# Input projection of the Mamba-2 layer: operand halves side by side, normalized inputs, half-size units, two evacuation queues

## The chip, the cores and the metric

One core of one Trainium2 chip runs the whole program in one launch. The metric is device microseconds (us) of one execution, the median of three runs.

## The reference, cut to what matters

A two-layer trunk on 256 tokens with width 2048. Layer 0 is a Mamba-2 mixer, layer 1 windowed attention, and each is followed by a SwiGLU FFN. The change touches only the first step of layer 0:

```python
h = rms_norm(x, mix_norm[0])          # x * rsqrt(mean(x*x) + eps) * gain
proj = h @ w_in                       # 2048 -> 10304
z   = proj[..., :4096]
xbc = silu(causal_depthwise_conv(proj[..., 4096:10240], conv_w, conv_b))   # x, B, C
dt  = softplus(proj[..., 10240:] + dt_bias)
# then per group (8 of them): SSD over 8 heads, y * silu(z), RMS norm, @ w_out
```

## The kernel before, in words

**Split arithmetic.** Each fp32 operand is held as a high part and a low part, and a product is the sum of high·high, high·low and low·high on TensorE (PE). Weights arrive in tiles of 128x2048; each half of a tile (128x1024) is split on the chip by `split` (L145): a ScalarE (ACT) cast makes `wh`, a VectorE (DVE) subtraction makes `wl`. Both have four buffers, and `next_half` (L160) issues splits three halves ahead of their use. A *half* below is one such piece and the matmuls that read it.

**Units.** A unit fills one of two accumulators `acc` (two PSUM banks each). `t_units` (L222) runs three passes over 256 columns: high weights on the activation's high part, on its low part, and low weights on the high part, 24 matmuls a half. `p_unit` (L250) streams high and low parts side by side, so that a high weight tile is loaded once for 512 columns: 8 matmuls of 512 (L261) and 8 of 256 (L265) a half. It leaves two sums that have to be added afterwards. The FFN and half of the output projection use `p_unit` already.

**Work behind the matmuls.** What follows a unit is a Python generator, put in a queue of `Background` (L43). After each half `step` (L68) advances the front generator of each queue by one piece, unless the work issued on DVE or ACT exceeds its allowance (1.3 and 1.4 us a half, by the kernel's own estimate); what exceeds it stays as a debt. The order of every engine's instructions is fixed by this when the program is built. `begin_unit` (L199) may have two units open: before a new one starts, `need` (L74) advances all queues, whatever the debt, until the unit two before it has been evacuated, so that its accumulator is free. Instructions issued there stand ahead of the new unit's matmuls, and on DVE and ACT ahead of the next split.

**The projection** (L633 to L643): per group g one unit for B and C (256 columns, 4 halves), one for x (512 columns, 8 halves), one for z (8 halves); in group 0 also dt (2 halves). The inputs `XT` are x times gain, without the RMS factor; `scaled` (L392) multiplies that factor `rb` in when it reads PSUM, so no evacuation can start before the norm of all inputs is known (`prep`, L377). `bc_evac`, `x_evac` and `z_evac` go to queue 0, `dt_evac` and `ssd` to queue 2, `ssd_norm` to queue 1.

Of the kernel before, what the change touches and what calls it, by code (L numbers as in the profile page):

```python
# [10 lines left out]
F32 = mybir.dt.float32  # L11
F32R = mybir.dt.float32r
AF = mybir.ActivationFunctionType
OP = mybir.AluOpType
# [71 lines left out]
def trunk_kernel(  # L86
# [41 lines left out]
    def bg_bank():  # L128
        return psum.tile([P, 512], F32, tag="bg", bufs=4, name=name("bg"))

    bg = Background(3, (V, A))


    n_tiles = weights.shape[0]
# [112 lines left out]
    def t_unit(ncols, X, xkey, evac, q=0):  # L247
        t_units([(0, range(16))], ncols, 16, X, xkey, [evac], q)

    def p_unit(nk, X, xkey, evac):  # L250


        u, ps = begin_unit()
        for k0 in range(0, nk, 4):
            h, l = next_half(256)
            ks = range(k0, k0 + 4)
            for k in ks:
                bg.need((xkey, k // 2))
            for k in ks:
                for m in range(2):  # L260
                    T.matmul(ps[:, m], h[:, k % 4, m * P:(m + 1) * P], X[k], start=(k == 0), stop=False,  # L261
                             skip_group_check=True)
            for k in ks:
                for m in range(2):
                    T.matmul(ps[:, m, 0], l[:, k % 4, m * P:(m + 1) * P], X[k][:, 0, :], start=False,  # L265
                             stop=(k == nk - 1), skip_group_check=True)
            bg.step()
        bg.add(0, evac(ps, u))

    def joined(ps):  # L270

# [105 lines left out]
    def prep():  # L377
        for nb in range(4):
            for pair in (2 * nb, 2 * nb + 1):
                gained(pair, 0)  # L380
            add_squares()
            for pair in (2 * nb, 2 * nb + 1):
                squares(pair)
            yield
        yield from finish_norm()
        V.tensor_scalar(cwb, cwb, 0.5, None, OP.mult)
        A.activation(hpar[64:128, 1:2], hpar[64:128, 1:2], AF.Exp)
        V.tensor_scalar(hpar[64:128, 1:2], hpar[64:128, 1:2], -1.0, None, OP.mult)
        V.memset(hpar[0:64, 1:2], 1.0)
        bg.done.add("prep")  # L390

    def scaled(sums):  # L392
        u = tmp([P, 2, S])
        V.tensor_tensor(u, sums, rb[:, None, :].to_broadcast([P, 2, S]), OP.mult)
        return u

    def dt_evac(ps, u):
        while "prep" not in bg.done:
            yield
        xb, e, r, q = (wide()[:, 0:S] for _ in range(4))  # L400
        V.tensor_tensor(xb, ps[:, 0, 0], rb, OP.mult)
        bg.done.add(("evac", u))
        A.activation(xb, xb, AF.Identity, bias=hpar[:, 0:1])
        A.activation(e, xb, AF.Abs)
        A.activation(e, e, AF.Exp, scale=-1.0)
        yield
        V.tensor_scalar(r, e, 2.0, None, OP.add)
        V.reciprocal(r, r)
        yield
        V.tensor_tensor(e, e, r, OP.mult)  # L410
        V.tensor_tensor(r, e, e, OP.mult)
        yield
        V.tensor_scalar(q, r, 1.0 / 19, None, OP.mult)
        for j, c in enumerate((17, 15, 13, 11, 9, 7, 5, 3)):
            V.scalar_tensor_tensor(q, q, 1.0 / c, r, OP.add, OP.mult)
            if j % 2:
                yield
        V.scalar_tensor_tensor(q, q, 1.0, e, OP.add, OP.mult)
        V.tensor_scalar(xb, xb, 0.0, None, OP.max)
        V.scalar_tensor_tensor(q, q, 2.0, xb, OP.mult, OP.add)  # L420
        V.tensor_scalar(q, q, hpar[:, 1:2], None, OP.mult)
        yield
        b = bg_bank()
        for tb in range(2):
            T.transpose(b[:, tb * P:(tb + 1) * P], q[:, tb * P:(tb + 1) * P], ident)
        yield
        bv = b[:, 0:256].rearrange("p (t d h) -> p t d h", d=2, h=64)
        an = tmp([P, 2, 64])
        V.tensor_copy(dtn, bv[:, :, 0, :])
        V.tensor_copy(an, bv[:, :, 1, :])  # L430
        yield
        b1, b2 = bg_bank(), bg_bank()
        for c in range(2):
            T.matmul(b1[0:64, c * P:(c + 1) * P], an[:, c, :], tri, start=(c == 0), stop=True, skip_group_check=True)
        for j, (lhs, c) in enumerate(((tri, 0), (tri2, 0), (tri, 1))):
            T.matmul(b2[:, j * 64:(j + 1) * 64], lhs, an[:, c, :], start=(j == 0), stop=True, skip_group_check=True)
        yield
        at = tmp([P, S])
        V.tensor_copy(at[0:64, :], b1[0:64, 0:256])
        nc.gpsimd.dma_start(acum, at[0:64, :])  # L440
        for j, sc in enumerate((1.0, -1.0, 1.0)):
            A.mul(bias3[:, j, :], b2[:, j * 64:(j + 1) * 64], sc)
        yield
# [11 lines left out]
                V.scalar_tensor_tensor(dst[:, m, d:], u[:, m, :S - d], cwb[:, j * 48 + ct:j * 48 + ct + 1],  # L455
                                       dst[:, m, d:], OP.mult, OP.add)

    def half_tanh(v, scale):
        th = tmp([P, 2, S])
        A.activation(th, v, AF.Tanh, scale=scale)  # L460
        return th

    def gate(out_, th, v):
        V.scalar_tensor_tensor(out_, th, 1.0, v, OP.add, OP.mult)

    def bc_evac(g):
        def gen(ps, u):
            v = scaled(ps[:, :, 0])
            bg.done.add(("evac", u))
            yield  # L470
            both, cts = slot([P, 1024]), (32 + g, 40 + g)
            bc = both[:, 0:512].rearrange("p (a t) -> p a t", t=S)
            first_tap(v, bc, cts)
            yield
            taps(v, bc, cts, (2, 1))
            yield
            taps(v, bc, cts, (0,))
            yield
            th = half_tanh(bc, 1.0)
            yield  # L480
            gate(bc, th, bc)
            BC[g] = bc, both[:, 512:896]
            yield
        return gen

    def x_evac(g):
        def gen(ps, u):
            xs = slot([P, 4, S])
            d0, d1 = xs[:, 0:2, :], xs[:, 2:4, :]
            c0, c1 = (4 * g, 4 * g + 1), (4 * g + 2, 4 * g + 3)  # L490
            v0 = scaled(ps[:, 0])
            yield
            first_tap(v0, d0, c0)
            v1 = scaled(ps[:, 1])
            bg.done.add(("evac", u))
            yield
            taps(v0, d0, c0, (2, 1))
            first_tap(v1, d1, c1)
            yield
            taps(v0, d0, c0, (0,))  # L500
            taps(v1, d1, c1, (2,))
            yield
            th = half_tanh(d0, 1.0)
            taps(v1, d1, c1, (1, 0))
            yield
            gate(d0, th, d0)
            th = half_tanh(d1, 1.0)
            yield
            gate(d1, th, d1)
            XS[g] = xs  # L510
            bg.add(2, ssd(g))
        return gen

    def z_evac(g):
        def gen(ps, u):
            sz = slot([P, 4, S])
            v0 = scaled(ps[:, 0])
            yield
            t0 = half_tanh(v0, 0.5)
            v1 = scaled(ps[:, 1])  # L520
            bg.done.add(("evac", u))
            yield
            gate(sz[:, 0:2, :], t0, v0)
            t1 = half_tanh(v1, 0.5)
            yield
            gate(sz[:, 2:4, :], t1, v1)
            SZ[g] = sz
        return gen

    BC, XS, SZ, Y = {}, {}, {}, {}  # L530

    def ssd(g):
# [31 lines left out]
        def gated(b):  # L564
            if gates[0] > b:
                return True
            if g not in SZ:
                return False
            sz = SZ[g] if b == 0 else SZ.pop(g)
            for i in range(2):  # L570
                p = 2 * b + i
                V.scalar_tensor_tensor(xs[:, p, :], xs[:, p, :], dsk[:, 4 * g + p:4 * g + p + 1],
                                       yb[b][:, i * S:(i + 1) * S], OP.mult, OP.add)
            G.tensor_tensor(xs[:, 2 * b:2 * b + 2, :], xs[:, 2 * b:2 * b + 2, :], sz[:, 2 * b:2 * b + 2, :], OP.mult)
            gates[0] += 1
            return True
# [28 lines left out]
            yield  # L605
        while not gated(1):
            yield
        bg.add(1, ssd_norm(g, xs))

    def ssd_norm(g, xs):  # L610
        sq = [tmp([P, 2, S]) for _ in range(2)]
        for b in range(2):
            A.activation(sq[b], xs[:, 2 * b:2 * b + 2, :], AF.Square)
        yield
# [15 lines left out]
            store(Y, 4 * g + 2 * i, t)  # L630
            bg.done.add(("Y", 2 * g + i))

    bg.add(0, prep())  # L633
    bg.need(("XT", 1))
    for g in range(NG):
        t_unit(256, XT, "XT", bc_evac(g))
        if g == 0:
            t_unit(128, XT, "XT", dt_evac, 2)
        t_unit(512, XT, "XT", x_evac(g))
        t_unit(512, XT, "XT", z_evac(g))  # L640
    bg.need("rstd")
    bg.need(("evac", units[0] - 1))
    clear_norm()  # L643
    t_units(OUT0, 512, 32, Y, "Y", [t_residual(nb, 32) for nb in (0, 1)])
    for pair in range(4, 8):
        p_unit(32, Y, "Y", p_residual(pair, 32))
# [255 lines left out]
def _weights(i):  # L902
# [15 lines left out]
    for g in range(NG):  # L918
        put(r16, (w_in, 8192 + g * P, P), (w_in, 9216 + g * P, P))
        if g == 0:  # L920
            put(r16, (w_in, 10240, 64), (w_in, 10240, 64))
        put(r16, (w_in, 4096 + g * 512, 512))
        put(r16, (w_in, g * 512, 512))

    def put_out(w, order, nk):
        for j, ks in order:
# [85 lines left out]
```

## Time and profile before

| | |
|---|---|
| median of 3 runs (range) | 2697.92 us (2697.36 to 2698.32) |
| the profiled execution | 2698.51 us |
| its span on the engines | 2696.4 us |
| PE, PE weight loads, DVE, ACT busy | 99%, 89%, 63%, 49% of the span |
| granted PE clock over the span | 0.999 of full speed |

The projection takes the first 0.5 ms or so, the output projection of layer 0 runs from about 570 to 632 us, and the FFN follows. Times in the rows are us from the start of the span; a matmul's row gives the time that it was in the engine, and since matmuls overlap, the pace is read from the starts.

### The profile page before, as it was taken

How to read it: one execution, taken by the hardware profiler on the slowest of the kernel's cores; microseconds unless marked ns; L12 is line 12 of the kernel's file. 1: busy time of each engine (PE TensorE's matmuls, PEld its weight loads, DVE VectorE, ACT ScalarE, POOL GpSimd, SP SyncE). 2: the span in 40 equal slices, each digit the busy share in tenths (PEclk: the TensorE clock that was granted, in tenths of full speed). 3: DMA queues.
4: the chain of work that ended last, by engine and by line, in shares of the span. 5: the costliest groups of instructions: out<-in, count | busy, mean ns of one | idle time of the engine just before them, and what ended most of it. 6: DMA issues, size and time to landing. Idle time of an engine off the chain costs nothing.

```text
span 2696.4 us, 40315 instructions
## 1 busy us (share of the span) xinstructions
PE 2673.5 (99%) x16460; PEld 2391.9 (89%) x16460; DVE 1700.7 (63%) x2104; ACT 1326.3 (49%) x1947; POOL 199.8 (7%) x215
## 2 busy tenths in 40 slices
PE   7999999999999999999999999999999999999999
PEld 7999999999888888888888888888888888888888
DVE  6777777756566666665555777766666666665444
ACT  5666666654454444444444555544454444444332
POOL 1011111110000000000001330220000000000000
PEclk9999999999999999999999999999999999999999
DMA  5454555545555555555555554553455555555553
GB/s 222 178 184 175 187 179 189 177 177 187 188 188 188 188 188 187 189 189 193 190 189 203 183 186 152 185 185 141 156 188 188 188 188 188 188 188 194 197 198 128
DMA packets 71432, 495.75 MB, mean 184 GB/s; under 512 B 8320, under 2 KB 8704, under 8 KB 13008
## 3 DMA queue, kind: packets, MB, share of 16 engines
q1 hardware_dynamic: 68400, 483.81, 49.5%
q0 software_dynamic: 2848, 9.37, 1.1%
q8 instruction: 129, 2.11, 0.3%
q14 instruction: 55, 0.45, 0.1%
HBM read 490.99 MB, written 2.16 MB: 183 GB/s over the span
## 4 chain that ended last, share of the span: by engine, by line
PE 98%; ACT 1%; issue 0%; DVE 0%; POOL 0%; DMA 0%; SPq 0%; ACTq 0%; POOLq 0%
PE acc L261 39%; PE acc L240 21%; PE acc L265 20%; PE acc L217 15%; PE bg L588 1%; PE bg L754 0%; PE bg L787 0%; PE bg L860 0%; PE bg L549 0%; ACT wh L38 0%; ACT slot L38 0%; PE bg L324 0%; PE bg L784 0%; PE bg L862 0%; DMA xres<-in_x_dram 0%
## 5 line engine op out<-in xcount | busy, mean ns | idle before, releaser
L38 DVE TENSOR_TENSOR wl<-w,wh 128x1024 fp32r<-128x1024 f32 x914 | 1128.3, 1236 | 904.7 <-ACT wh L38 903.7
L38 ACT CAST wh<-w 128x1024 fp32r<-128x1024 f32 x914 | 955.5, 1047 | 1089.8 <-PE acc L261 507.2
L261 PE MATMUL acc<-slot,wh 128*128 128x512 f32 x4416 | 1106.7, 392 | 2.1 <-DVE xres L38 1.7
L261 PEld LDWEIGHTS acc<-slot,wh 128*128 128x128 f32 x4416 | 794.2, 189 | 145.1 <-issue 2.7
L265 PEld LDWEIGHTS acc<-slot,wl 128*128 128x128 f32 x4416 | 602.4, 190 | 43.0
L265 PE MATMUL acc<-slot,wl 128*128 128x256 f32 x4416 | 615.7, 282 | 0.0
L240 PE MATMUL acc<-slot,wh 128*128 128x256 f32 x3232 | 430.1, 286 | 12.8 <-ACT wh L38 10.7
L240 PEld LDWEIGHTS acc<-slot,wh 128*128 128x128 f32 x3232 | 404.8, 193 | 19.9 <-ACT wh L38 10.8
L217 PE MATMUL acc<-wh,slot 128*128 128x512 f32 x1152 | 290.5, 394 | 0.0
L217 PEld LDWEIGHTS acc<-wh,slot 128*128 128x128 f32 x1152 | 213.7, 188 | 43.2
L240 PE MATMUL acc<-slot,wl 128*128 128x256 f32 x1616 | 226.8, 283 | 0.9 <-DVE wl L38 0.9
L240 PEld LDWEIGHTS acc<-slot,wl 128*128 128x128 f32 x1616 | 208.6, 192 | 1.1 <-DVE wl L38 1.1
L217 PE MATMUL acc<-wl,slot 128*128 128x512 f32 x576 | 154.2, 389 | 0.0
L217 PEld LDWEIGHTS acc<-wl,slot 128*128 128x128 f32 x576 | 108.1, 188 | 22.7
L38 ACT ACTIVATE tmp<-tmp 128x256 f32<-128x256 f32 (+1 forms) x104 | 46.8, 450 | 163.9 <-DVE tmp L38 163.6
L284 POOL TENSOR_TENSOR tmp<-tmp 128x256 f32<-128x256 f32 x32 | 27.6, 868 | 1022.1 <-ACT tmp L38 1017.0
L38 ACT ACTIVATE wide<-tmp,bias 128x128 f32<-128x128 f32 x192 | 62.9, 391 | 13.9 <-PE bg L588 9.4
L38 DVE SCALAR_TENSOR_TENSOR slot<-tmp,vec,slot 128x255 f32<-128x255 f32 (+1 forms) x144 | 67.6, 528 | 0.0
L38 DVE TENSOR_TENSOR tmp<-tmp 128x256 f32<-128x256 f32 x88 | 37.4, 425 | 42.6 <-ACT tmp L38 42.6
L38 DVE TENSOR_TENSOR tmp<-acc,tmp 128x512 f32<-128x512 f32 x88 | 60.1, 683 | 4.0 <-ACT tmp L38 4.0
L38 DVE TENSOR_TENSOR tmp<-tmp,rb 128x512 f32<-128x512 f32 x88 | 60.3, 686 | 0.1
L38 ACT ACTIVATE tmp<-slot 128x128 f32<-128x128 f32 (+1 forms) x136 | 52.7, 394 | 14.9 <-DVE slot L38 13.8
(131 smaller groups left out, 1191.3 us busy)
## 6 DMA issues: line engine op xcount, KB each, us to landing
w<-in_weights_dram SPq DMA_DIRECT2D x455, 1024.0 KB, 4.8
tmp<-acum POOLq DMA_DIRECT2D x32, 256.0 KB, 4.6
xres<-in_x_dram SPq DMA_DIRECT2D x4, 512.0 KB, 7.8
w<-in_weights_dram SPq DMA_DIRECT2D x4, 512.0 KB, 8.4
out_dram<-xres SPq DMA_DIRECT2D x8, 256.0 KB, 2.2
slot<-in_mask_dram POOLq DMA_DIRECT2D x1, 384.0 KB, 5.6
slot<-in_q_norm_dram POOLq DMA_DIRECT2D x1, 192.0 KB, 5.6
slot<-in_k_norm_dram POOLq DMA_DIRECT2D x1, 192.0 KB, 7.5
```

The costliest lines, as they stand in the source:

```text
L38: return call(out, *args, **kw)
L217: T.matmul(ps[tb], X[k][:, part, tb * P:(tb + 1) * P], w[:, k % 2, :], start=(k == 0 and i == 0), stop=(k == 15 and i == 2))
L240: T.matmul(pss[j][:, b, c, :], w[:, k % kk, m * P:(m + 1) * P], X[k][:, part, :], start=(k == 0 and i == 0 and c == 0), stop=(k == nk - 1 ...
L261: T.matmul(ps[:, m], h[:, k % 4, m * P:(m + 1) * P], X[k], start=(k == 0), stop=False, skip_group_check=True)
L265: T.matmul(ps[:, m, 0], l[:, k % 4, m * P:(m + 1) * P], X[k][:, 0, :], start=False, stop=(k == nk - 1), skip_group_check=True)
L284: G.tensor_tensor(sq[:, 0, :], sq[:, 0, :], sq[:, 1, :], OP.add)
L588: T.matmul(o[:, tb * P:], xdt[:, tb, q * 64:(q + 1) * 64], m[:, 256 * tb:256 + 128 * tb], start=(tb == 0 and q % 4 < 2), stop=(tb == 1), s ...
```

## The change

- The projection's units become `p_unit`s of 256 columns, 4 halves each: per group B/C, x first half, z first half, x second half, z second half. dt stays a `t_unit`. The weights are packed in that order.
- For groups 1 to 7 the operands are `XN`: x·gain·rb, made by a new generator `normed` after `prep`. Only group 0 still reads `XT` and multiplies by `rb` when it is evacuated.
- `total` takes a unit out of PSUM: an ACT copy of the second sum, and, one step later, a DVE addition of the first. `conv` holds the convolution, one engine's work in each step. `z_evac` has one step for the tanh and one for the product.
- B/C and z evacuations go to a fourth queue (number 3), x evacuations to queue 0, `prep` to queue 1. `ssd_norm` squares into z's buffer instead of two temporary ones.

```diff
-    bg = Background(3, (V, A))
+    bg = Background(4, (V, A))
...
-        bg.add(0, evac(ps, u))
+        bg.add(q, evac(ps, u))
...
+    def normed():
...
+            if j >= 2:
+                v, t = vs.pop(j - 2), ts.pop(j - 2)
+                V.tensor_tensor(t[:, :, 1, :], v, t[:, :, 0, :].bitcast(F32), OP.subtract)
...
+            if 1 <= j < 9:
+                ts[j - 1] = operand()
+                A.copy(ts[j - 1][:, :, 0, :], vs[j - 1])
+            if j < 8:
+                v = vs[j] = tmp([P, 2, S])
+                for i in range(2):
+                    k = 2 * j + i
+                    V.scalar_tensor_tensor(v[:, i, :], xt[:, k, :], gains[:, k:k + 1], rb, OP.mult, OP.mult)
+            yield
+
+    def total(ps, u, g):
+        v = tmp([P, 2, S])
+        A.copy(v, ps[:, :, 1])
+        yield
+        V.tensor_tensor(v, ps[:, :, 0], v, OP.add)
+        bg.done.add(("evac", u))
+        if g == 0:
+            while "prep" not in bg.done:
+                yield
+            V.tensor_tensor(v, v, rb[:, None, :].to_broadcast([P, 2, S]), OP.mult)
+        yield
+        return v
...
     def dt_evac(ps, u):
+        xb, e, r, q = (wide()[:, 0:S] for _ in range(4))
+        A.copy(xb, ps[:, 0, 0])
+        bg.done.add(("evac", u))
         while "prep" not in bg.done:
             yield
...
+    def conv(u, dst, cts):
+        first_tap(u, dst, cts)
+        yield
+        taps(u, dst, cts, (2, 1))
+        yield
+        taps(u, dst, cts, (0,))
+        yield
+        A.activation(u, dst, AF.Tanh)
+        yield
+        gate(dst, u, dst)
...
     for g in range(NG):
-        t_unit(256, XT, "XT", bc_evac(g))
+        X, key = (XT, "XT") if g == 0 else (XN, "XN")
+        p_unit(16, X, key, bc_evac(g), 3)
         if g == 0:
             t_unit(128, XT, "XT", dt_evac, 2)
-        t_unit(512, XT, "XT", x_evac(g))
-        t_unit(512, XT, "XT", z_evac(g))
-    bg.need("rstd")
+        for i in range(2):
+            p_unit(16, X, key, x_evac(g, i))
+            p_unit(16, X, key, z_evac(g, i), 3)
```

How the instructions move is seen at two places. Halves are counted from 1 through the projection, 162 in all. Names with numbers are buffers: `acc_65`, `acc_82` and `acc_108` are the units of halves 11 to 14, 15 to 18 and 19 to 22 after the change, `wl` the low weights of a half, `slot_79` and `slot_100` convolution results, `wide` values of the dt chain, `rb` the RMS factor.

DVE before, in the middle of the second unit of 512 columns (halves 15 to 22), where the dt chain ends:

```order
L38 TENSOR_TENSOR wl_83_683<-w_67_548,wh_82_682 128x1024
L38 TENSOR_TENSOR tmp_84_712<-acc_50_384,rb_97 128x512
L38 SCALAR_TENSOR_TENSOR wide_49_379<-wide_49_379,wide_47_377 128x256
L38 TENSOR_SCALAR wide_46_376<-wide_46_376 128x256
L38 SCALAR_TENSOR_TENSOR wide_49_379<-wide_49_379,wide_46_376 128x256
L38 TENSOR_SCALAR wide_49_379<-wide_49_379,vec_77 128x256
L38 TENSOR_TENSOR wl_86_719<-w_67_548,wh_85_718 128x1024
L38 SCALAR_TENSOR_TENSOR slot_79_675<-tmp_80_676,vec_77,slot_79_675 128x255 x2
L38 SCALAR_TENSOR_TENSOR slot_79_675<-tmp_80_676,vec_77,slot_79_675 128x254 x2
L38 TENSOR_TENSOR wl_89_755<-w_73_614,wh_88_754 128x1024
```

DVE with the change, the end of what `need` issues ahead of half 19 (the 44 instructions from the split of half 21 to the addition that empties `acc_65`), and what follows:

```order
L38 SCALAR_TENSOR_TENSOR slot_100_669<-tmp_47_335,slot_100_669 128x512
L38 SCALAR_TENSOR_TENSOR wide_46_333<-wide_46_333,wide_44_331 128x256
L38 TENSOR_SCALAR wide_43_330<-wide_43_330 128x256
L38 SCALAR_TENSOR_TENSOR wide_46_333<-wide_46_333,wide_43_330 128x256
L38 TENSOR_SCALAR wide_46_333<-wide_46_333,vec_77 128x256
L38 SCALAR_TENSOR_TENSOR slot_79_545<-tmp_97_659,slot_79_545 128x512
L38 TENSOR_TENSOR tmp_106_720<-acc_65_449,tmp_106_720 128x512
L38 TENSOR_TENSOR tmp_106_720<-tmp_106_720,rb_97 128x512
L38 TENSOR_TENSOR wl_110_730<-w_76_523,wh_109_729 128x1024
L38 TENSOR_TENSOR wl_113_752<-w_85_579,wh_112_751 128x1024
L38 TENSOR_TENSOR wl_115_772<-w_85_579,wh_114_771 128x1024
```

Before, two to five instructions stand between one split and the next. With the change 45 stand between the splits of halves 21 and 22, and then eight splits follow each other.

PE with the change, from the end of half 18 into half 19:

```order
L265 MATMUL acc_82_554<-slot_27_222,wl_84_556 128x256 x4
L265 MATMUL acc_82_554<-slot_28_227,wl_84_556 128x256 x4
L456 MATMUL bg_107_723<-cm_75,wide_46_333 128x128 x2
L261 MATMUL acc_108_728<-slot_4_101,wh_86_581 128x512 x4
L261 MATMUL acc_108_728<-slot_5_106,wh_86_581 128x512 x4
L265 MATMUL acc_108_728<-slot_4_101,wl_87_582 128x256 x4
```

Half 19 writes the accumulator that `acc_65` held, and stands behind the transposes (L456) of the dt chain's last `wide_46`.

ACT with the change, what `need` issues ahead of half 31 (`acc_140` is the unit of halves 27 to 30, `acc_119` that of 23 to 26, which half 31 waits for):

```order
L38 CAST wh_149_1001<-w_127_876 128x1024
L38 COPY tmp_151_1021<-acc_140_936 128x512
L38 COPY slot_100_669<-bg_137_921 128x128
L38 ACTIVATE slot_131_901<-tmp_135_917 128x512
L38 ACTIVATE wide_154_1033<-tmp_136_919,bias3_99 128x128 x3
L38 ACTIVATE wide_154_1033<-wide_154_1033 128x384
L38 ACTIVATE slot_155_1039<-tmp_151_1021,vec_77 128x256 x2
L38 ACTIVATE wide_156_1043<-tmp_136_919,bias3_99 128x128 x3
L38 ACTIVATE wide_156_1043<-wide_156_1043 128x384
L38 COPY tmp_158_1050<-acc_119_813 128x512
```

The copy of the unit that has just ended now stands first, and the copy that frees the accumulator last.

## Rows read from the trace of the kernel before

**Rows 1.** The page: busy time of the engines and its share of the span.

```profile
PE 2673.5 (99%) x16460; PEld 2391.9 (89%) x16460; DVE 1700.7 (63%) x2104; ACT 1326.3 (49%) x1947; POOL 199.8 (7%) x215
```

**Rows 2.** Stretches: length, busy PE, PEld, DVE, ACT, POOL, clock, DMA share, GB/s.

```profile
300.00:360.00 60.00, 60.00 (x500) 58.09 (x499) 46.17 (x69) 36.39 (x61) 10.04 (x11) 1.00 0.51 183
700.00:900.00 200.00, 200.00 (x1147) 176.01 (x1146) 123.30 (x144) 95.32 (x125) 3.60 (x5) 1.00 0.51 185
```

**Rows 3.** PE's timeline in the projection: start, us; two halves of 24 matmuls.

```profile
42.11 2.08 PE L240 MATMUL acc<-slot,wh 128*128 128x256 f32 x16
44.99 2.08 PE L240 MATMUL acc<-slot,wh 128*128 128x256 f32 x16
```

**Rows 4.** The timeline in the FFN: two starts of a half, and a split.

```profile
699.02 1.05 ACT L38 CAST wh<-w 128x1024 fp32r<-128x1024 f32 x1 [1.74 <-PE acc L261]
699.77 2.00 PE L261 MATMUL acc<-slot,wh 128*128 128x512 f32 x8
700.10 1.23 DVE L38 TENSOR_TENSOR wl<-w,wh 128x1024 fp32r<-128x1024 f32 x1 [1.57 <-ACT wh L38]
...
702.56 2.00 PE L261 MATMUL acc<-slot,wh 128*128 128x512 f32 x8
```

**Rows 5.** The timeline where the norm of the inputs is awaited.

```profile
31.72 0.51 PE L311 MATMUL bg<-ones,rb 128*128 128x2 f32 x4
...
34.57 1.22 PE L324 MATMUL bg<-tmp,ones 128*128 128x256 f32 x2 [2.35 <-POOL tmp L321]
...
36.72 0.69 DVE L38 TENSOR_TENSOR tmp<-acc,rb 128x512 f32<-128x512 f32 x1
...
37.56 3.75 PE L240 MATMUL acc<-slot,wh 128*128 128x256 f32 x16 [1.77 <-DVE tmp L38]
```

**Rows 6.** Stretches inside and behind that pause; the clock is third from the end.

```profile
33.00:34.00 1.00, 0.00 (x0) 0.00 (x0) 0.00 (x0) 0.00 (x0) 0.90 (x3) 1.00 0.98 393
38.00:39.00 1.00, 1.00 (x7) 1.00 (x7) 0.00 (x0) 0.94 (x3) 0.00 (x0) 0.50 0.00 0
```

**Rows 7.** Groups of DVE: count, busy us, mean ns, idle before.

```profile
L38 DVE SCALAR_TENSOR_TENSOR slot<-tmp,vec,slot 128x255 f32<-128x255 f32 (+1 forms) x144 | 67.6, 528 | 0.0
L38 DVE TENSOR_TENSOR wide<-wide,slot 128x384 f32<-128x384 f32 x64 | 35.2, 550 | 0.0
L38 DVE TENSOR_TENSOR tmp<-acc,rb 128x512 f32<-128x512 f32 x40 | 27.3, 683 | 1.5 <-PE acc L240 1.5
L38 DVE SCALAR_TENSOR_TENSOR slot<-slot,vec,bg 128x256 f32<-128x256 f32 x64 | 27.0, 474 | 0.0
L38 DVE SCALAR_TENSOR_TENSOR wide<-wide,wide 128x256 f32<-128x256 f32 x10 | 4.2, 422 | 0.2
L38 DVE TENSOR_TENSOR slot<-bg,cm 128x128 f32<-128x128 f32 x16 | 3.9, 282 | 0.0
```

**Rows 8.** Groups of ACT; the copy is the FFN's.

```profile
L38 ACT ACTIVATE wide<-tmp,bias 128x128 f32<-128x128 f32 x192 | 62.9, 391 | 13.9 <-PE bg L588 9.4 <-DMA tmp<-acum 4.4
L38 ACT ACTIVATE wide<-wide 128x384 f32<-128x384 f32 x64 | 33.6, 526 | 2.0
L38 ACT ACTIVATE slot<-tmp,vec 128x256 f32<-128x256 f32 x48 | 26.2, 593 | 0.0
L38 ACT COPY tmp<-acc 128x512 f32<-128x512 f32 x88 | 51.0, 580 | 5.3 <-PE acc L265 5.3
```

**Rows 9.** PE's timeline around background matmuls of the SSD.

```profile
275.37 0.60 PE L544 MATMUL bg<-slot 128*128 128x256 f32 x2
...
276.82 2.15 PE L240 MATMUL acc<-slot,wh 128*128 128x256 f32 x16
...
300.44 0.87 PE L588 MATMUL bg<-wide,slot 128*64 128x256 f32 x8
301.24 2.17 PE L240 MATMUL acc<-slot,wh 128*128 128x256 f32 x16
```

**Rows 10.** The page, DMA issues: count, KB each, us from issue to landing.

```profile
tmp<-acum POOLq DMA_DIRECT2D x32, 256.0 KB, 4.6
```

More of the change, by code (lines that the diff above doesn't have):

```diff
@@ L248, in t_unit, with p_unit @@
         t_units([(0, range(16))], ncols, 16, X, xkey, [evac], q)
-    def p_unit(nk, X, xkey, evac):
+    def p_unit(nk, X, xkey, evac, q=0):
         u, ps = begin_unit()
@@ L266, in p_unit @@
                              stop=(k == nk - 1), skip_group_check=True)
-            bg.step()
-        bg.add(0, evac(ps, u))
+            bg.step(units[0] == 1)
+        bg.add(q, evac(ps, u))
     def joined(ps):
@@ L390, in prep @@
         bg.done.add("prep")
[L392 to L395, printed above, removed]
+        bg.add(1, normed())
+    XN = {}
+    def normed():
+        vs, ts = {}, {}
+        for j in range(10):
+            if j >= 2:
+                v, t = vs.pop(j - 2), ts.pop(j - 2)
+                V.tensor_tensor(t[:, :, 1, :], v, t[:, :, 0, :].bitcast(F32), OP.subtract)
+                store(XN, 2 * (j - 2), t)
+                bg.done.add(("XN", j - 2))
+            if 1 <= j < 9:
[19 more added lines that the diff above has]
+        return v
     def dt_evac(ps, u):
+        xb, e, r, q = (wide()[:, 0:S] for _ in range(4))
+        A.copy(xb, ps[:, 0, 0])
+        bg.done.add(("evac", u))
         while "prep" not in bg.done:
             yield
-        xb, e, r, q = (wide()[:, 0:S] for _ in range(4))
-        V.tensor_tensor(xb, ps[:, 0, 0], rb, OP.mult)
-        bg.done.add(("evac", u))
+        V.tensor_tensor(xb, xb, rb, OP.mult)
         A.activation(xb, xb, AF.Identity, bias=hpar[:, 0:1])
@@ L456, in taps @@
                                        dst[:, m, d:], OP.mult, OP.add)
[L458 to L461, printed above, removed]
     def gate(out_, th, v):
         V.scalar_tensor_tensor(out_, th, 1.0, v, OP.add, OP.mult)
+    def conv(u, dst, cts):
[8 more added lines that the diff above has]
+        gate(dst, u, dst)
     def bc_evac(g):
         def gen(ps, u):
[L468 to L471, printed above, removed]
+            v = yield from total(ps, u, g)
+            both = slot([P, 1024])
             bc = both[:, 0:512].rearrange("p (a t) -> p a t", t=S)
[L473 to L481, printed above, removed]
+            yield from conv(v, bc, (32 + g, 40 + g))
             BC[g] = bc, both[:, 512:896]
@@ L484, in bc_evac, with x_evac, z_evac, gen @@
         return gen
-    def x_evac(g):
+    def x_evac(g, i):
         def gen(ps, u):
[L488 to L491, printed above, removed]
-            yield
-            first_tap(v0, d0, c0)
-            v1 = scaled(ps[:, 1])
-            bg.done.add(("evac", u))
+            v = yield from total(ps, u, g)
+            if i == 0:
+                XS[g] = slot([P, 4, S])
+            yield from conv(v, XS[g][:, 2 * i:2 * i + 2, :], (4 * g + 2 * i, 4 * g + 2 * i + 1))
+            if i == 1:
+                bg.add(2, ssd(g))
+            yield
+        return gen
+    def z_evac(g, i):
+        def gen(ps, u):
+            v = yield from total(ps, u, g)
+            if i == 0:
+                sz[g] = slot([P, 4, S])
+            z = sz[g][:, 2 * i:2 * i + 2, :]
+            A.activation(z, v, AF.Tanh, scale=0.5)
             yield
-            taps(v0, d0, c0, (2, 1))
-            first_tap(v1, d1, c1)
+            gate(z, z, v)
+            if i == 1:
+                SZ[g] = sz.pop(g)
             yield
[L500 to L511, printed above, removed]
-        return gen
[L514 to L528, printed above, removed]
+        return gen
+    sz = {}
     BC, XS, SZ, Y = {}, {}, {}, {}
@@ L568, in gated @@
                 return False
-            sz = SZ[g] if b == 0 else SZ.pop(g)
+            sz = SZ[g]
             for i in range(2):
@@ L607, in ssd, with ssd_norm @@
             yield
-        bg.add(1, ssd_norm(g, xs))
-    def ssd_norm(g, xs):
-        sq = [tmp([P, 2, S]) for _ in range(2)]
+        bg.add(1, ssd_norm(g, xs, SZ.pop(g)))
+    def ssd_norm(g, xs, sq):
+        sq = [sq[:, 0:2, :], sq[:, 2:4, :]]
         for b in range(2):
@@ L631, in ssd_norm @@
             bg.done.add(("Y", 2 * g + i))
-    bg.add(0, prep())
+    bg.add(1, prep())
     bg.need(("XT", 1))
     for g in range(NG):
-        t_unit(256, XT, "XT", bc_evac(g))
+        X, key = (XT, "XT") if g == 0 else (XN, "XN")
+        p_unit(16, X, key, bc_evac(g), 3)
         if g == 0:
             t_unit(128, XT, "XT", dt_evac, 2)
-        t_unit(512, XT, "XT", x_evac(g))
-        t_unit(512, XT, "XT", z_evac(g))
-    bg.need("rstd")
+        for i in range(2):
+            p_unit(16, X, key, x_evac(g, i))
+            p_unit(16, X, key, z_evac(g, i), 3)
+        if g == 0:
+            XT.clear()
     bg.need(("evac", units[0] - 1))
     clear_norm()
+    XN.clear()
     t_units(OUT0, 512, 32, Y, "Y", [t_residual(nb, 32) for nb in (0, 1)])
@@ L921, in _weights @@
             put(r16, (w_in, 10240, 64), (w_in, 10240, 64))
-        put(r16, (w_in, 4096 + g * 512, 512))
-        put(r16, (w_in, g * 512, 512))
+        for i in range(2):
+            put(r16, (w_in, 4096 + g * 512 + i * 256, 256))
+            put(r16, (w_in, g * 512 + i * 256, 256))
     def put_out(w, order, nk):
```

## The prediction

> **What bounds the kernel now.** I read the page first: PE is busy for 99% of the span, DVE for 63% and ACT for 49% [rows 1]. DVE and ACT matter only where PE has to wait for them. Then the stretches: in the projection (300 to 360 us) PE is busy for all of 60 us at the full clock, DVE for 46 of 60 and ACT for 36 [rows 2]. So the stage is paced by PE, and the question is what one half costs there now and after the change, and whether PE will have to wait.
>
> The pace comes from two timelines. A half of three passes takes 44.99 - 42.11 = 2.88 us [rows 3]; a side-by-side half, as the FFN runs it, takes 702.56 - 699.77 = 2.79 us [rows 4]. The columns streamed are the same (24 x 256 against 8 x 512 + 8 x 256); only weight loads go away.
>
> The last thing to read is how far DVE runs ahead of PE. In the FFN the split three halves ahead ends at 700.10 + 1.23 = 701.33, and the half in progress ends at 702.56 [rows 4]: it could not be earlier, since the ACT cast before it waited for PE to release a buffer. So DVE reaches work that stands behind that split **1.23 us before PE finishes its half**. Splits are covered by three halves; work issued between two units is covered by this 1.23 us alone if the next unit's matmuls wait for it.
>
> **The change, part by part.**
>
> *Pace.* 156 halves of the projection change form (160, less four at the start, which wait for inputs in both kernels): 156 x (2.88 - 2.79) = **-14 us**. Here a rule can be weighed. Weight loads are busy for 58.1 of 60 us in the projection and 176 of 200 in the FFN [rows 2], and the FFN's row of the very same form gives 2.79. The Trainium skill (Perfetto Trace Analysis, Identifying the Most-Contended Engine) holds that the share of weight loads, not of matmuls, tells how near PE is to its limit. By that rule 16 loads in place of 24 would make a half 2.88 x 16/24 = 1.92 us and the stage 150 us shorter. The row of the same form decides, and I take -14.
>
> *Start.* Before, the first x unit waits for the whole chain of the norm: its matmuls of row sums at 31.72, the spreading matmul at 34.57, the scaling on DVE at 36.72, first matmul at 37.56, and those 16 matmuls take 3.75 us instead of 2.08 [rows 3, 5]. With the change the first unit is emptied by a copy and an addition that need no factor; the addition stands behind the small DVE operation after the row sums, so PE goes on at about 31.72 + 0.51 + 0.2 + 0.69 = 33.1. That is 4.4 us, and 1.7 more since the clock should not fall: **-6 us**.
>
> *Evacuation.* Units are half as long, so the unit that `need` wants empty ended only four halves (11 us) ago, and all B/C and z evacuations share one queue of some 15 steps a group. In group 0 the new `normed` (24 DVE instructions), the dt chain and two convolutions exceed the allowance, steps are withheld, and at the start of half 19 z's first evacuation stands behind an unfinished B/C one. `need` then issues everything at once. The order shows it: 44 DVE instructions between the split of half 21 and the addition that empties the accumulator of half 19. Their debt withholds the steps of the next units, so that `need` has to issue those too. I count 13 such unit starts, ahead of halves 19, 27, 31, 39, 47, 51, 59, 67, 71, 79, 87, 91 and 99; from half 103 on the DVE work between two splits is as thin as before.
>
> The DVE work that PE must wait for there, 217 instructions: 62 of 512 columns or PSUM by 0.683, 66 taps by 0.528, 28 by 0.550, 34 by 0.474, 12 by 0.422, and 15 small ones by 0.282 us [rows 7], **118 us** in all. By unit start: 22.6, 2.7, 7.2, 13.3, 5.9, 7.9, 15.1, 4.7, 9.7, 12.1, 5.9, 4.3, 6.7. Less 1.23 us each, 102 us. The six multiplications of `normed` among them have no row before; they lie between 0.422 (rows in scratch) and 0.683 (twice the columns), and I take 0.474, which also reads a scalar, a tensor and a factor: 1 us either way.
>
> At some starts ACT is the longer path, because the copy of the unit that has just ended stands first on it and cannot begin before PE is done. Ahead of half 31: copy 0.58, a small copy about 0.3, tanh taken as the copy, 3 x 0.391 + 0.526 = 1.7, two taps 1.19, again 1.7, copy 0.58, and 0.68 for DVE's addition, 7.3 us [rows 7, 8], where DVE alone gives 6.0. The same sum for the starts at 27, 31, 51, 67, 71 and 91, and small PE matmuls in the chain at 47 and 87, adds some 9.5 us: pauses of 21.4, 2.9, 7.4, 12.1, 4.9, 8.8, 13.9, 4.8, 8.8, 10.8, 5.0, 5.3, 5.4, together **+111.5 us**. Bounds: 102 if only DVE counts; with DVE and ACT never side by side (86 us of ACT stand in the same places), 188. I stay near the lower end, since each queue's ACT step is followed by other queues' DVE steps.
>
> *What PE does in the pauses.* 13 batches of four L588 matmuls take 301.24 - 300.44 = 0.80 us each and four groups of transposes 276.82 - 275.37 = 1.45 us [rows 9]; with dt's and the norms' small ones, 19 us. They were PE time before and now lie inside the pauses: **-19 us**.
>
> *Clock.* In the one pause of this stage PE stood without work in 33 to 34, and behind it the granted clock was 0.50 (1.2 of 2.4 GHz) [rows 6]; the first 16 matmuls cost 3.75 - 2.08 = 1.67 us more [rows 3, 5]. Twelve of the pauses are longer: 12 x 1.67 = **+20 us**; 0 if the small matmuls inside keep the clock up. The Trainium skill (Perfetto Trace Analysis, Matmul Optimizations) also speaks against breaking up the stream: it wants matmuls back to back, since the engine's power follows its use.
>
> *No cost.* The ACT copies (5 of 0.58 us a group [rows 8]) and additions that take the place of scalings lie in the 14 and 24 us that DVE and ACT have free in a stretch of 60 [rows 2]; without that cover they are part of the pauses, where they are counted. The SSD's fetches on POOL's queue move with its steps; each is issued two heads ahead of its use and lands in 4.6 us [rows 10], so where both steps fall into one pause ACT can wait for it once a group: nothing to 5 x 4.6 = 23 us, and I take nothing and leave that end to the range. Weight transfers and the FFN are untouched. The squares of `ssd_norm` only change their buffer.
>
> Sum: +111.5 - 19 + 20 - 14 - 6 = **+92 us** on the profiled execution's 2698.5 us, so 2791; the median of the runs lies 0.6 us under that execution: **2790 us**. A measurement tells 0.2% (5 us) from no change.
>
> **Rivals.**
>
> *The evacuations are hidden after all (faster).* If DVE and ACT reached that work earlier than PE ends its half, by more than its length, the change would keep its pace and start: 2698 - 20 = 2678 us. For it: DVE is idle for a quarter of the stage [rows 2], and two accumulators are there for this. Against: the cast and the split wait for a buffer that PE releases, so idle time lies ahead of the split, not behind it; it decides at 1.23 us, and all 13 sums are over it. Chance 0.05. By the Trainium skill (Perfetto Trace Analysis, Matmuls), groups that rotate through PSUM banks overlap their evacuation, and larger matmuls are more efficient; that would be this case.
>
> *DVE and ACT take turns (slower still).* A generator's steps alternate between the engines, and `need` runs them back to back, so each could wait for the other: 188 us of pauses, 76 more than taken, 2867 us. Against: three or four generators advance in each round, so that between two steps of one there are those of the others; ahead of half 19 that is a norm's, a dt's, an x's and a z's. Chance 0.09.
>
> *Weight loads set the pace.* 1.92 us a half (above): 2790 + 14 - 150 = 2654 us. Against it stands the FFN's own pace. Chance 0.01. The change does do what it says in the code; that a queue then forces the steps together is the order's doing.
>
> **How the numbers follow.** The forecast has 0.84, alternation 0.09, hidden 0.05, weight loads 0.01; 0.01 is left for pauses that just offset the gains. Low end: pauses 102, no clock loss: 102 - 19 - 20 = +63, 2761, and a little for rounding. High end: the forecast with the fetches' 23 us and 13 us, a sixth of the way to alternation: 2826. Outside lie the rivals and a small tail. Faster 0.06, within 0.2% 0.01, slower 0.93.
>
> **What the profile after would show.** Halves of about 2.79 us between pauses. PE idle ahead of halves 19, 31, 39, 59, 71 and 79, the first about 20 us long, ended by a DVE operation that reads `acc` or by DVE results for small matmuls; the clock at 0.5 behind them; no long pause after about 400 us. PE's idle time in the first half millisecond near 90 us in place of the few at the start. If the pauses are missing, or PE's wait is on `wh` or `wl`, the argument on the buffer is wrong; if they are twice as long with DVE idle inside, it is the alternation.

## The result, and the profile after

| | before | after |
|---|---|---|
| median (range) | 2698.12 us (2697.36 to 2698.89) | 2766.52 us (2765.72 to 2767.30) |
| span of the profiled execution | 2696.4 us | 2765.5 us |
| granted PE clock over the span | 0.999 | 0.985 |

The change makes the kernel 2.5% slower: ratio 1.0253, 95% interval 1.0241 to 1.0265. The forecast was 2790 us, slower, with a range from 2761, "and a little for rounding", to 2826. Nearly all of the loss arises in the projection: its last half ends 67.6 us later than before (603.21 in place of 535.61 us), of the 69.1 us by which the span grew.

The page's busy line and four stretches, columns as in [rows 1, 2]:

```profile
PE 2687.4 (97%) x15180; PEld 2340.7 (85%) x15180; DVE 1723.0 (62%) x2133; ACT 1348.4 (49%) x1996; POOL 206.3 (7%) x215
```

```profile
60.00:80.00 20.00, 6.67 (x41) 5.80 (x39) 19.83 (x42) 8.93 (x14) 0.00 (x0) 0.72 0.26 102
80.00:100.00 20.00, 14.30 (x72) 12.36 (x73) 13.09 (x22) 6.25 (x7) 0.00 (x0) 0.77 0.29 106
300.00:360.00 60.00, 47.91 (x268) 41.56 (x267) 36.87 (x52) 26.90 (x41) 10.31 (x11) 0.88 0.43 155
400.00:460.00 60.00, 60.00 (x357) 51.59 (x358) 49.44 (x71) 40.79 (x72) 14.04 (x13) 1.00 0.50 178
```

From 60 to 80 us PE works a third of the time and DVE all of it; at 300 to 360, where PE was busy for 60 of 60 us [rows 2], it is busy for 48. From 400 to 460 us it is full again. What PE waited for between 40 and 620 us, by the list of waits (total us, times, longest):

```profile
PE bg L456 <- DVE wide L38: 19.0, 1, 19.0
PE bg L597 <- DVE wide L38: 14.0, 12, 2.0
PE bg L311 <- POOL slot L625: 13.1, 3, 9.1
PE acc L261 <- DVE tmp L38: 11.3, 8, 3.2
```

The first row is the pause ahead of half 19: the transposes of the dt chain (L456) stand first there, as the order showed. L597 and L311 are background matmuls that `need` put ahead of a unit, L261 is the unit's own first matmul: only this last row is a wait for the addition that empties an accumulator. The row on POOL was in no term of the forecast.

Between pauses the pace is that of the FFN, and the start is earlier. PE's timeline, first two halves in a row, then the norm of the inputs, which answers to [rows 3, 5]:

```profile
49.75 2.00 PE L261 MATMUL acc<-slot,wh 128*128 128x512 f32 x8
...
52.55 2.00 PE L261 MATMUL acc<-slot,wh 128*128 128x512 f32 x8
```

```profile
31.83 0.50 PE L311 MATMUL bg<-ones,rb 128*128 128x2 f32 x4
32.45 2.11 PE L261 MATMUL acc<-slot,wh 128*128 128x512 f32 x8
...
38.15 0.59 PE L324 MATMUL bg<-tmp,ones 128*128 128x256 f32 x2
```

A half takes 52.55 - 49.75 = 2.80 us (2.793 on average over the 75 halves that nothing holds up), and the first x unit starts at 32.45 in place of 37.56 us: it no longer waits for the spreading matmul (L324), which now stands ahead of half 9.

The clock behind a pause: stretches inside the first pause, just behind it and one half later, and the first matmuls behind it.

```profile
70.00:72.00 2.00, 0.00 (x0) 0.00 (x0) 1.97 (x5) 0.54 (x2) 0.00 (x0) 0.50 0.00 0
...
86.00:89.00 3.00, 3.00 (x9) 2.42 (x8) 2.67 (x4) 0.00 (x0) 0.00 (x0) 0.50 0.00 0
90.00:92.00 2.00, 2.00 (x12) 1.74 (x12) 1.23 (x1) 0.72 (x1) 0.00 (x0) 1.00 0.80 324
```

```profile
85.70 0.69 PE L456 MATMUL bg<-cm,wide 128*128 128x128 f32 x2 [19.03 <-DVE wide L38]
86.04 3.59 PE L261 MATMUL acc<-slot,wh 128*128 128x512 f32 x8
```

Behind the pause the granted clock stands at 0.50 (1.2 of 2.4 GHz), and the eight matmuls of 512 columns take 3.59 us in place of 2.00; a half later it is at 1.00.

### The profile page after: what moved, and what is told of

Same layout as the page of the kernel before. It is cut to its first block, busy times and chain, and to the rows that moved or that the text cites. A ratio compares the mean times of both kernels' runs of the same rounds, so it can differ in the third digit from the quotient of the medians.

```text
span 2765.5 us, 37806 instructions
## 1 busy us (share of the span) xinstructions
PE 2687.4 (97%) x15180; PEld 2340.7 (85%) x15180; DVE 1723.0 (62%) x2133; ACT 1348.4 (49%) x1996; POOL 206.3 (7%) x215
## 4 chain that ended last, share of the span: by engine, by line
PE 94%; DVE 3%; ACT 2%; issue 1%; POOL 0%; DMA 0%; SPq 0%; DVEq 0%; POOLq 0%; ACTq 0%
PE acc L261 48%; PE acc L265 24%; PE acc L217 14%; PE acc L240 4%; DVE slot L38 2%; ACT wide L38 1%; PE bg L597 1%; DVE wl L38 1%; DVE wide L38 0%; ACT wh L38 0%; DVE tmp L38 0%; ACT slot L38 0%; PE bg L767 0%; PE bg L800 0%; PE bg L873 0%
## 5 line engine op out<-in xcount | busy, mean ns | idle before, releaser
L261 PE MATMUL acc<-slot,wh 128*128 128x512 f32 x5696 | 1449.5, 397 | 24.9 <-DVE tmp L38 11.3
L261 PEld LDWEIGHTS acc<-slot,wh 128*128 128x128 f32 x5696 | 1035.9, 191 | 218.7 <-issue 11.7
L265 PEld LDWEIGHTS acc<-slot,wl 128*128 128x128 f32 x5696 | 781.0, 191 | 57.8 <-DVE wl L38 1.3
L265 PE MATMUL acc<-slot,wl 128*128 128x256 f32 x5696 | 797.1, 283 | 0.9 <-DVE wl L38 0.9
L38 ACT ACTIVATE tmp<-tmp 128x256 f32<-128x256 f32 x88 | 36.7, 418 | 163.5 <-DVE tmp L38 163.5
L38 DVE TENSOR_TENSOR tmp<-acc,tmp 128x512 f32<-128x512 f32 x128 | 87.5, 684 | 9.8 <-ACT tmp L38 9.8
L240 PE MATMUL acc<-slot,wh 128*128 128x256 f32 x672 | 88.5, 285 | 0.0
L38 ACT COPY tmp<-acc 128x512 f32<-128x512 f32 x128 | 74.0, 579 | 25.0 <-PE acc L265 25.0
L240 PEld LDWEIGHTS acc<-slot,wh 128*128 128x128 f32 x672 | 83.7, 191 | 0.9 <-issue 0.7
L38 DVE SCALAR_TENSOR_TENSOR slot<-tmp,vec,slot 128x254 f32<-128x254 f32 (+2 forms) x144 | 72.3, 558 | 0.0
L583 POOL TENSOR_TENSOR slot<-slot,slot 128x512 f32<-128x512 f32 x16 | 26.1, 1631 | 339.0 <-DVE slot L38 299.0
```

Of the source, the lines that this page charges most:

```text
L38: return call(out, *args, **kw)
L240: T.matmul(pss[j][:, b, c, :], w[:, k % kk, m * P:(m + 1) * P], X[k][:, part, :], start=(k == 0 and i == 0 and c == 0), stop=(k == nk - 1 ...
```

## The experiments

All were compared with the kernel before on their own chip, whose median there was 2698.3 to 2698.6 us. Two theories stood against each other. The **queue theory** is the forecast's: the withheld steps, which `need` forces together ahead of a unit, cost the time. The **form theory** says that half-size units, their copies and additions cost it whatever the order.

**Steps never withheld.** The rule of debts is switched off for the projection, all else is the change.

```diff
-            bg.step(units[0] == 1)
+            bg.step(units[0] <= 41)
...
     clear_norm()
+    bg.debt = [0.0, 0.0]
```

> The changed kernel, with one thing altered: in the projection every step advances every queue whatever the debt (and the debt is cleared behind it). All instructions stay; only their order changes. No unit start then has forced evacuations, except 3.7 us of DVE work ahead of half 19. Queue theory (withheld steps force the work together): the pauses go, the gains of pace and start stay, and DVE is only overloaded in halves 15 to 22 (about 39 us of work in 22 us of PE time, 8 of the difference covered by the splits ahead): 2698 - 20 + 12 = about 2690 us. Form theory (twice as many units, each with a copy and an addition, are more than DVE and ACT can carry, however queued): the work is the same, so 2755 or more.

Measured: 2698.02 us, ratio 0.9999 (0.9990 to 1.0009). The whole loss of 68 us is gone with one condition: the form theory falls. The wanted gain did not come either, because one pause is left, ahead of half 19. PE's timeline there:

```profile
82.39 3.75 PE L261 MATMUL acc<-slot,wh 128*128 128x512 f32 x8 [14.22 <-DVE tmp L38]
```

In group 0 DVE really has more to do than fits (the dt chain, `normed` and the convolutions), and the addition that frees the accumulator stands behind that backlog: 16.1 us from start to start beyond a half, where I had counted 12, and 2.4 for the clock. Another 2.6 us go behind the projection, in the first halves of the output projection: the projection itself ends 2.6 us earlier than before (533.05 against 535.61). Hence 2698 and not 2690.

**z in a queue of its own**, debts kept.

```diff
-    bg = Background(4, (V, A))
+    bg = Background(5, (V, A))
...
-            p_unit(16, X, key, z_evac(g, i), 3)
+            p_unit(16, X, key, z_evac(g, i), 4)
```

> The changed kernel with z evacuations in a queue of their own (five queues), debt as it is. The DVE work forced ahead of unit starts falls from 118 to 49 us. Queue theory, with the price that the changed kernel showed (90 us of pauses and 17 of clock for 118 us of forced DVE work at 13 starts): pauses of about 31 us, clock 9, so about 2707 us. Form theory: as the changed kernel, 2755 or more, since no work goes away.

Measured: 2710.74 us, ratio 1.0043 (1.0027 to 1.0059). The queue theory had 2707. 56 of the 68 us return although debts still withhold steps. An evacuation that has a queue to itself stands behind fewer unfinished ones, so less is forced.

**The opposite: x, z and B/C all in queue 0**, debts kept.

```diff
-        p_unit(16, X, key, bc_evac(g), 3)
+        p_unit(16, X, key, bc_evac(g))
...
-            p_unit(16, X, key, z_evac(g, i), 3)
+            p_unit(16, X, key, z_evac(g, i))
```

> The changed kernel with x, z and B/C evacuations all in queue 0, as before the change. Forced DVE work is 111 us up to half 99 and goes on to the last group, some 155 us in all at about 25 starts. Queue theory: pauses of about 110 us and clock of 25, less the small matmuls inside them: about 2783 us, with pauses still there at 550 us. If two queues are themselves the trouble: faster than the changed kernel's 2766.

Measured: 2836.58 us, ratio 1.0513 (1.0492 to 1.0534): the direction held, the number was 54 us too low. PE's waits from 40 to 620 us:

```profile
PE acc L261 <- DVE tmp L38: 38.2, 22, 2.8
PE bg L456 <- DVE wide L38: 19.9, 1, 19.9
PE bg L324 <- POOL tmp L321: 18.4, 6, 4.1
```

Pauses go on to the last group, and a part of them is again a wait on POOL, which a count of DVE's work alone leaves out.

**Steps never withheld, and no `normed`.** As the first experiment; all groups read `XT` and multiply `rb` in when they are evacuated.

```diff
-        bg.add(1, normed())
...
-        if g == 0:
+        if True:
             while "prep" not in bg.done:
...
-        X, key = (XT, "XT") if g == 0 else (XN, "XN")
+        X, key = XT, "XT"
...
-        if g == 0:
-            XT.clear()
```

> As the run with steps never withheld, but without the normalized operands: all groups read x times gain, and the RMS factor is multiplied in after each evacuation (40 more DVE multiplications in all, 24 fewer of the operand generator's). Queue theory: no forced work, and DVE's overload in halves 15 to 22 shrinks to some 8 us: 2698 - 20 + 4 = about 2682 us. If the normalized operands carry a gain of their own (less DVE work per group): slower than the run that has them.

Measured: 2688.96 us, ratio 0.9965 (0.9952 to 0.9978), faster than both kernels, though not the 2682 of the queue theory. Of the pause ahead of half 19 there remain 6.2 us, and 1.9 for the clock; 3.3 go in the first halves of the output projection:

```profile
72.91 3.74 PE L261 MATMUL acc<-slot,wh 128*128 128x512 f32 x8 [6.03 <-DVE tmp L38]
```

**No `normed`, debts kept** (the diff above without the first experiment's).

> The change without `normed`: all groups read XT and multiply rb after the evacuation, the rule of debts stays. Theory A (it is `normed`, with the dt chain, that starts the debts, as the prediction put it): without its 24 DVE instructions and 8 ACT copies the forced work should shrink clearly; with 77 us of forced DVE work at the starts up to half 99 in place of 118, about 2757 us. Theory B (the shared queue and the rule of debts force the steps, whoever made the debt): by the order the extra multiplication by rb in each evacuation keeps the queue full, and work is forced at 24 starts up to the last group, 139 us of DVE in all; between the change with 118 us at 13 starts (2767) and the one-queue kernel with 155 us at 25 starts (2837), so about 2800 us.

Measured: 2775.02 us, ratio 1.0281 (1.0267 to 1.0295). Neither number is met, but theory A's sign is wrong: without `normed` the kernel is 8.5 us slower than the change. Pauses now come in every group, up to the one ahead of half 159. PE's waits from 40 to 620 us:

```profile
PE bg L311 <- POOL slot L624: 43.8, 6, 8.5
PE acc L261 <- DVE tmp L38: 15.4, 9, 2.4
```

The largest wait here is the one on POOL, in the forced norms; neither theory had a term for it.

The four kernels form a square:

| | debts kept | steps never withheld |
|---|---|---|
| with `normed` | 2766.5 us | 2698.0 us |
| without | 2775.0 us | 2689.0 us |

The rule of debts costs 68.5 us in one row and 86 in the other; `normed` makes about 9 us, of either sign.

**The norm passed over by `need`.** The change, with `ssd_norm` in a fifth queue that `need` leaves alone when it waits for an accumulator.

```diff
-            for q in self.queues:
-                self.advance(q)
+            for n, q in enumerate(self.queues):
+                if n != 4 or key[0] != "evac":
+                    self.advance(q)
...
-        bg.add(1, ssd_norm(g, xs, SZ.pop(g)))
+        bg.add(4, ssd_norm(g, xs, SZ.pop(g)))
```

> The change, with `ssd_norm` in a fifth queue that `need` passes over when it waits for an accumulator; all else as in the change, rule of debts included. In the change PE waits 13.1 us on POOL's result at three unit starts (halves 47, 79, 119), since `need` forces the whole norm of a group ahead of the next unit. Theory A (the forced work is paid for wherever it stands, on POOL too): these three waits and the norm's part of DVE's forced work go; by the order 89 us of DVE work stay forced at the 13 starts in place of 118, so 13 us and three quarters of 29 us less, and some clock: about 2730 us, 2720 to 2745. Theory B (DVE's work alone is paid for and POOL's lies beside it): 22 us less, about 2744 us with no change of the pauses at 47, 79 and 119 beyond that. If the norm only moves to other unit starts: no gain, 2760 to 2770 us.

Measured: 2748.59 us, ratio 1.0184 (1.0167 to 1.0201), 18 us less than the change and a little above what either theory gave. PE's waits from 40 to 620 us (lines stand one further down in this kernel, so that L262 and L598 are L261 and L597 above):

```profile
PE acc L262 <- DVE tmp L38: 18.2, 11, 3.7
PE bg L598 <- DVE wide L38: 11.3, 9, 2.7
```

The wait on POOL is gone. At the three unit starts where it stood, the pause and the half behind it together took beyond their pace 8.6, 14.0 and 4.0 us in the change and take 4.2, 5.7 and 1.7 here, 15.0 us less. The other starts give 3 us in all, but not start by start: ahead of halves 71 and 87, where no wait on POOL stood, 13.4 us went, and at others, 83 and 143 among them, some 11 came on balance. So my three quarters for the 29 us of DVE work were too much in the sum. That the forced norm costs time is shown; how much of it is POOL's part is not, since its DVE and ACT steps left the same places.

**Two ways on from the fastest version.** Both start from the kernel with steps never withheld and no `normed`. One gives z a queue of its own; the other keeps the rule of debts for queue 2 alone (dt chain and SSD):

```diff
-        for q in self.queues:
-            if free or all(
+        for n, q in enumerate(self.queues):
+            if free and n != 2 or all(
```

> Steps never withheld, no `normed`, and z's evacuations in a queue of their own (five queues). In the version with four queues one pause was left, 6.2 us and 1.9 us of slow clock at half 18 to 19, where DVE's backlog of the dt chain and the convolutions of group 0 stands ahead of the addition that frees the accumulator. A queue more lets that addition go 4 places earlier, but puts more steps into each round: if the place in the queue decides, the pause shrinks to 2 to 4 us, 2684 to 2687 us; if DVE's total work in group 0 decides, it stays, 2689 us.

> Steps never withheld except in queue 2 (dt chain and SSD), which keeps the rule of debts; no `normed`; four queues. If DVE's backlog in group 0 is the cause of the last pause at half 18, the dt chain is now spread over later halves and the pause goes, 8 us less than the version with all steps free: 2681 us. Against it: SSD steps come later and may pile up at the start of the output projection, where a few us more would be lost: then 2685 to 2695 us.

Measured: 2685.15 us, ratio 0.9952 (0.9940 to 0.9965), and **2683.40 us, ratio 0.9945 (0.9932 to 0.9959)**, the fastest of all. The first lies in the range given for "the place in the queue decides": the pause ahead of half 19 is down to 1.1 us, and 3.1 are lost in the half behind it. In the second, between its two forecasts, the pause is down to 2.5 us, with 1.6 behind it for the clock:

```profile
65.52 1.11 PE L265 MATMUL acc<-slot,wl 128*128 128x256 f32 x8
68.96 3.21 PE L261 MATMUL acc<-slot,wh 128*128 128x512 f32 x8 [2.32 <-DVE tmp L38]
```

This is the rival "hidden after all" (2678 us) but for 5 us: the projection ends 17.9 us earlier than before (517.71 against 535.61), and 3.3 of these go again in the output projection. So the new form does bring its pace and its start, once no evacuation is held back; `normed` is no part of it.

## Why the prediction was right, point by point

The measured column is read from PE's timeline, from the start of each half to that of the next, less 2.793 us (2.88 in the old form). A pause in it is all that the next half starts late by, small matmuls in between included.

| term | forecast, us | measured, us |
|---|---|---|
| pace | -14 | -13.4: 155 halves, from half 8 on, by 2.880 - 2.793 |
| start | -6 | -6.8: half 8 starts at 35.35, before at 42.11 |
| 13 pauses | +111.5 | +90.2 |
| a pause not forecast, ahead of half 119 | 0 | +2.3 |
| clock behind the pauses | +20 | +16: 19.1 in the halves behind them, less 3.1 in the same places before |
| small matmuls now inside pauses | -19 | -18.4: beyond the pace outside the pauses 23.2, before 41.6 |

Less 2.4 us that stood before at the places of the pauses, the measured terms give +67.5 us, against 67.6 read at the projection's end; the median grew by 68.4.

The **mechanism** was right: steps forced ahead of a unit's start, with PE standing behind them. Each of the 13 starts came late, by length in us (forecast, measured): half 19 21.4, 19.5; 27 2.9, 3.3; 31 7.4, 3.4; 39 12.1, 9.9; 47 4.9, 6.4; 51 8.8, 6.3; 59 13.9, 9.4; 67 4.8, 4.7; 71 8.8, 7.0; 79 10.8, 11.6; 87 5.0, 5.1; 91 5.3, 1.6; 99 5.4, 2.0. PE had no matmul at all for 56.8 of the 90.2 us; the rest is small matmuls, and at 27, 91 and 99 they are most of the delay (idle 0.2, 0.6 and 0.5 us). So one sign failed: by the busy lines PE's idle time is 2765.5 - 2687.4 = 78.1 us in place of 22.9 over the whole span, 55 more and not near 90. The small matmuls took 33 us inside the pauses, where the forecast had the 19 that they take between halves. A part of this is the clock: from 157.8 to 162.8 us, in the pause ahead of half 39, the granted clock is 0.50 as well.

The **term that was mis-sized** is the pauses, 111.5 us, and of it the point where the sum ends. It runs to the last forced addition on DVE at every start. The timelines at the start of half 31, of PE, DVE and ACT:

```profile
127.97 3.75 PE L261 MATMUL acc<-slot,wh 128*128 128x512 f32 x8 [3.25 <-DVE tmp L38]
```

```profile
127.15 0.68 DVE L38 TENSOR_TENSOR tmp<-acc,tmp 128x512 f32<-128x512 f32 x1
...
130.90 0.69 DVE L38 TENSOR_TENSOR tmp<-acc,tmp 128x512 f32<-128x512 f32 x1
```

```profile
130.29 0.57 ACT L38 COPY tmp<-acc 128x512 f32<-128x512 f32 x1
```

PE goes on when the first addition is done (127.15 + 0.68 = 127.83). That one empties `acc_140`, the unit that has just ended, since the copy of `acc_119`, the last in the order, begins only at 130.29; that copy and its addition run beside half 31. So half 31 writes the accumulator of `acc_140`, not that of `acc_119`, as the text on the order of ACT has it. In the same way half 19 starts at 86.04 us, before the addition that empties `acc_65` begins (86.16): it waited for the transposes, and not for that addition. At seven starts (31, 39, 51, 59, 71, 91 and 99) the half begins 2.5 to 5.6 us before the last forced addition ends, 23.8 us together. There the forecast was 61.7 us and the time measured 39.6; at the other six it was 49.8 against 50.7.

Up to the last addition the sum was near, 111.5 forecast against 114.7 measured, and that is partly luck, since four errors cancel. The 217 instructions last 123.2 us and not 118. Back to back they take 14.1 less than that. DVE is idle for 17.0 us among them, waiting mostly for ACT, where 9.5 were added for ACT and PE. And DVE reaches the work 11.4 us ahead of PE in all, not 13 x 1.23 = 16: its first forced instruction starts about 1.3 us before PE's half ends at ten starts, and no earlier than that end at halves 19, 31 and 99. How back-to-back instructions overlap is seen in DVE's timeline in the first pause:

```profile
75.44 0.68 DVE L38 TENSOR_TENSOR slot<-tmp,slot 128x512 fp32r<-128x512 f32 x1
76.04 0.87 DVE L38 SCALAR_TENSOR_TENSOR tmp<-xres,vec,rb 128x256 f32<-128x256 f32 x2
76.83 0.88 DVE L38 SCALAR_TENSOR_TENSOR wide<-wide,wide 128x256 f32<-128x256 f32 x2
77.63 2.45 DVE L38 SCALAR_TENSOR_TENSOR slot<-tmp,vec,slot 128x253 f32<-128x253 f32 x6
79.99 0.69 DVE L38 TENSOR_TENSOR slot<-tmp,slot 128x512 fp32r<-128x512 f32 x1
...
86.16 0.68 DVE L38 TENSOR_TENSOR tmp<-acc,tmp 128x512 f32<-128x512 f32 x1
```

An instruction of 0.68 us is followed by the next 0.60 us later, a pair of 0.87 takes 0.79, and six taps are through in 79.99 - 77.63 = 2.36 us, 0.39 each, where I took 0.528. The trace before showed it too, with four taps in 1.66 us:

```profile
69.73 1.66 DVE L38 SCALAR_TENSOR_TENSOR slot<-tmp,vec,slot 128x255 f32<-128x255 f32 x4
```

For PE I had read starts, not durations; for DVE I should have done the same.

At four of the six starts where the ACT term was added (31, 51, 71 and 91) 30.3 us were forecast and 18.3 measured. All four are among the seven starts above: at half 31 the copy that was to end ACT's chain begins at 130.29, when PE has long gone on. Two of the three waits on POOL, 12.1 us ahead of halves 47 and 79, stand in the measured pauses without a term of their own; the third is ahead of 119.

The **clock** loss came at the predicted size a pause, 1.0 to 2.5 us each (1.9 on average, forecast 1.67), but behind nine of the twelve: in halves 67, 91 and 99 the granted clock stayed at 1.00. The length of the delay alone does not decide: half 67 came 4.7 us late and lost nothing behind it, half 31 came 3.4 us late and lost 2.5. Behind the one at 119, not forecast, 1.7 us were lost. The **fetches** of the SSD ([rows 10]) cost PE no wait of their own, as taken; ACT waited for one once, for 1.4 us. **Weight loads** do not set the pace: the half takes 2.79 to 2.80 us and not 1.92, as [rows 4] had it, so a price of the half by its number of loads, as weighed there, does not hold for this stage. **Alternation** did not occur in the first pause: in 60 to 80 us DVE was busy for 19.83 of 20. In the later ones there is some of it, the 17.0 us above, far from the 76 of that rival. One reason was too simple: I named `normed` as what starts the debts, and the kernel without it is no faster while debts withhold steps.

## What to carry to other kernels

When the order of instructions is fixed at build time, ask of each buffer that is awaited what else must be issued before its release: a budget that holds work back only moves it to the place where all engines wait for it. End the sum of a pause at the instruction that lets PE go on, which need not be the last one issued there. Work it out from the starts of back-to-back instructions, not from the mean durations of groups, and include every engine that the forced steps touch. The same operand form cost 68 us or nothing by the rule of the queues alone, and brought 15 with `normed` left out as well.

## What the runs showed of the hardware that was not expected

PE's wait on POOL, the longest pause but one, ahead of half 79. PE, then DVE, then POOL, by their timelines:

```profile
317.77 1.52 PE L597 MATMUL bg<-wide,slot 128*64 128x256 f32 x16
328.37 1.01 PE L311 MATMUL bg<-ones,slot 128*128 128x2 f32 x4 [9.07 <-POOL slot L625]
```

```profile
323.45 0.68 DVE L38 SCALAR_TENSOR_TENSOR slot<-tmp,slot 128x512 f32<-128x512 f32 x1
324.05 4.93 DVE L38 SCALAR_TENSOR_TENSOR slot<-tmp,vec,slot 128x255 f32<-128x255 f32 x6
```

```profile
323.68 1.57 POOL L583 TENSOR_TENSOR slot<-slot,slot 128x512 f32<-128x512 f32 x1 [3.38 <-DVE slot L38]
325.99 1.46 POOL L624 TENSOR_TENSOR slot<-slot 128x512 f32<-128x512 f32 x1 [0.74 <-ACT slot L38]
327.53 0.79 POOL L625 TENSOR_TENSOR slot<-slot 128x256 f32<-128x256 f32 x1
```

POOL's product, ACT's squares and POOL's two sums follow each other, and PE's small L311 stands ahead of the unit. Meanwhile DVE needs 4.93 us for six taps that took 2.45 in the first pause, where POOL did nothing. POOL's product also takes longer, 1.63 us on average against 1.30 before. The Trainium skill (SBUF — State Buffer, Who interferes with whom) says that a DVE instruction with two SBUF inputs contends with a GpSimd instruction that reads SBUF; these rows agree. It also lies in the 0.528 us of [rows 7]: in the trace before, the 129 taps with no POOL instruction beside them take 0.466 to 0.481 us, and the 15 with one beside them 0.99 on average and up to 1.516; in the trace after it is 120 taps of 0.467 to 0.485 and 24 of 0.97 on average. No run here took POOL's work away, so the price of the contention alone stays open.
